# Gate and up of the feed-forward network in two blocks of 512 token pairs instead of three of 346 or 348, with the 32 sample tokens as separate fp32 products

## The chip, the cores and the metric

One core of one Trainium2 chip runs the whole program in a single launch. The metric is the device time of that launch in microseconds (us). Five engines work side by side, each with its own queue of instructions in a fixed order: PE (TensorE, the matrix multiplier; its weight loads are listed apart as PEld), ACT (ScalarE), DVE (VectorE), POOL (GpSimd), and SP, which here issues the DMA transfers. SBUF is the on-chip memory that all of them read, with 128 partitions; PSUM holds what PE writes; DRAM is the large memory outside, reached by DMA alone.

## The reference

One layer of an encoder is applied to 2048 prompt tokens and, with the same weights, to 32 sample tokens. All data are fp32, the model width is 1024, the hidden width of the feed-forward network 2816.

```
xp = xp + rmsnorm(mix_output(band_attention, gated_linear_attention))      # stage 1
xp = xp + rmsnorm(mem_attention(rmsnorm(xp)))                              # stage 2, 256 memory tokens
xp = xp + rmsnorm(swiglu(rmsnorm(xp, g_pre_ffn), w_gate, w_up, w_down))    # stage 3
swiglu(h) = (silu(h @ w_gate) * (h @ w_up)) @ w_down
```

The sample tokens go through the same three lines with cached keys, values and state. The change is in stage 3 and in the part of stage 2 that hands its result over.

## The kernel before

[...]

**Seven products.** The large products are made by a scheme with seven half-size products in place of eight: tokens are paired (a column of the operand is one token of the first half and one of the second), the width of 1024 is cut into two halves of 512, and seven sums of quarters (`seven_mov` for the tokens, `seven_sta` for the weights) are multiplied and added up. One unit is 7 products x 4 blocks of 128 rows x 3 = 84 matmuls, with as many columns as the block has token pairs.

**The stages by PE.** From 0 to about 151 us the first weights and tokens, to 545 us the combined projection, to 1159 us attention, gated recurrence and output projection, to 1387 us the memory scores (`ms`), to 1574 us the memory output (`mem_out`, PSUM tiles `mops`, four blocks of 512 tokens, weights `vw0` to `vw3`), to 2474 us gate and up (`gate_up`, PSUM tiles `pg_X`, `pg_Y`, `pg_Z` and `pu_X`, `pu_Y`, `pu_Z`), and then the down projection (`pdn`).

**Gate and up.** There are 1024 prompt pairs and 16 sample pairs. They go in three blocks (`CF = (348, 346, 346)`), and in each block over 11 groups `g` of 256 hidden columns. `unit_w` loads 1 MB of raw weights, forms the seven sums and splits them into 7 tiles (`wg_s` or `wu_s`); `unit` multiplies them with the block's seven operands `mf` and adds up on ACT and DVE; then silu, the product of both halves, and seven sums `u` for the down projection, which go to DRAM (`ud`). The operands of a block come from four raw tiles in SBUF (`hr`, the pool `cg`), which `ffn_raw` fills from DRAM: block 0 from already normed tokens (`h2d`), blocks 1 and 2 from `x2d`, multiplied by the gain and the row scale `r2d` on DVE. `ffn_ops` then makes the seven sums on DVE and splits each (cast 128x1384 on ACT, subtraction on DVE). Each `mf` tile exists once, so the next block's operand is written when the last product with the old one is done.

**Down.** `pdn` multiplies the seven sums `u` (tiles `ur`, 1 MB each, read from `ud`, split in place by `split_own`) in two halves of 512 pairs. The sample tokens' down products are plain fp32 products: `tail_down` takes the 32 tokens as weights of 32 columns, and four such matmuls stand side by side in PE (PSUM tile `utp`, line 2551).

**mem_out.** It norms its result twice (`n3` after the product, `n4` ahead of the network). For blocks 0 to 2 the squares are added up on DVE and one fp32 matmul with a matrix of ones sums over the partitions (line 2140); for block 3 (`BYTOK = 3`) each of the eight squares goes through such a matmul itself (line 2151).

**Order.** `Order` records all instructions, gives each a cost, and makes a plan by list scheduling in 60 passes; the plan sets the order on every engine, SP included, for the whole program. `shifted` moves a group's urgency, `whole` keeps PE instructions together.

**Addresses.** In the built program all weight tiles of gate and up and of down start 128 bytes past a multiple of 256 in their partition, the `ur` tiles on a multiple of 256, the rows of the `mf` tiles (348 x 4 bytes) at varying offsets. In `mem_out` the tiles `vw1` to `vw3` and all operands lie on multiples of 256; `vw0` lies 64 bytes past one.

Of the kernel before, what the change touches and what calls it, by code (L numbers as in the profile page):

```python
# [19 lines left out]
P = 128  # L20
# [28 lines left out]
class Order:  # L49
# [56 lines left out]
    def _cost(self, ins, kind, eng, outs, inps):  # L106

        n = self._free(outs[0])
        if eng == "PE":
# [10 lines left out]
            t = n * 0.4385 + 6.5  # L120
# [370 lines left out]
def encoder_step(ctx, tc, ins, outs):  # L491
# [16 lines left out]
    EARLY = 20000.0  # L508
    ident = cpool.tile([P, P], F32, name="ident")
# [115 lines left out]
    FIRST = 696  # L625
    h2d = [dpool.tile([D, min(n, FIRST - c0)], F32, name=f"h2d{b}") for b, (c0, n) in enumerate(CB) if c0 < FIRST]
    r2d = dpool.tile([P, T - FIRST], F32, name="r2d")
# [1192 lines left out]
    with ExitStack() as ph:  # L1820
# [273 lines left out]
        BYTOK = 3  # L2094

        def mem_out(b):
# [29 lines left out]
            def norm(name):  # L2126

                r = rs[0][:, 512 * (name == "n4") :][:, :n]
                if b >= BYTOK:
                    return norm_rows(name, r)  # L2130
                acc = row(f"{name}_{b}_acc")
# [9 lines left out]
                ACT.activation(r, ps, AF.Ln, bias=eps_t, scale=1.0 / D)  # L2141
                ACT.activation(r, r, AF.Exp, scale=-0.5)
                return r

            def norm_rows(name, r):

                ps = pn.tile([P, 512], F32, tag="norm", name=f"{name}_{b}_ps")
                for k in range(KT):
                    sq = copied(f"{name}_{b}_sq{k}")
                    ACT.activation(sq, y[k], AF.Square)  # L2150
                    PE.matmul(ps, lhsT=ones, rhs=sq, start=k == 0, stop=k == KT - 1)
# [19 lines left out]
            def fin_sample():  # L2171
                r = sample_norm("n3")
                xr = sample_small("xr_s").rearrange("p (k t) -> p k t", k=KT)
                SP.dma_start(xr, x1d[b][:, 512:].rearrange("(k p) t -> p k t", p=P))
# [3 lines left out]
                SP.dma_start(x2d[b][:, 512:].rearrange("(k p) t -> p k t", p=P), ys)  # L2178
                SP.dma_start(r2d[:, TP - FIRST :], sample_norm("n4"))

            def fin():
# [10 lines left out]
                hn = max(0, min(n, FIRST - s))  # L2192
                if hn < n:
                    SP.dma_start(r2d[:, s + hn - FIRST : s + n - FIRST], r[:, hn:])
                for k in range(KT):
                    if hn:
                        DVE.scalar_tensor_tensor(out=y[k][:, :hn], in0=y[k][:, :hn], scalar=gains["g_pre_ffn"][:, k : k + 1], in1=r[:, :hn], op0=ALU.mult, op1=ALU.mult)
                        SP.dma_start(h2d[b][k * P : (k + 1) * P, :], y[k][:, :hn])

            return [first] + ([fin_sample] if b == NB - 1 else []) + [partial(tile_m, m) for m in range(KT)] + [fin]  # L2200

        for b in range(NB):
            for it in mem_out(b):
                it()


    CF = (348, 346, 346)
    UN = 512
    TAIL = 330
    CTOK = [[[(0, 348)], [(348, 696)]], [[(696, 1042)], [(1042, 1388)]],  # L2210
            [[(1388, 1718), (TP, TP + 16)], [(1718, TP), (TP + 16, T)]]]
    CPUT = [[(0, 0, 348, 0)], [(0, 0, 164, 348), (1, 164, 346, 0)], [(1, 0, TAIL, 182)]]
# [6 lines left out]
    WRB, SGB = 4, 4  # L2219
    fps = ctx.enter_context(ExitStack())  # L2220
    pd, pt, pn = (fps.enter_context(tc.tile_pool(name=name, bufs=bufs, space=PSUM, **RW)) for name, bufs in (("cpd", 6), ("cpt", 1), ("cpn", 1)))
    with ExitStack() as ph:
# [3 lines left out]
        mps = {i: pool(f"cm{i}", 1) for i in (1, 2, 3, 4)}  # L2226
        sp = pool("cs", 4)
        mps[0] = pool("cm0", 1)
        gp = pool("cg", 4)
        wr = pool("cwr", WRB)  # L2230
        wsa = pool("cwa", 6)
        mps.update({i: pool(f"cm{i}", 1) for i in (5, 6)})
        wsb = pool("cwb", 6)

        def stage(name):
            return gp.tile([P, HK, 348], F32, tag="stage", name=name)

        scales = []

        def ffn_raw(b):  # L2240

            n = CF[b]
            raw, rows_ = {}, {}
            for kh, c in ((0, 0), (0, 1), (1, 1), (1, 0)):
                r = stage(f"hr{b}_{kh}{c}")
                at = 0
                for t0, t1 in CTOK[b][c]:
                    for bb, lo, hi, off in pieces(CB, t0, t1):
                        SP.dma_start(r[:, :, at + off : at + off + hi - lo], (x2d if b else h2d)[bb][kh * 512 : kh * 512 + 512, lo:hi].rearrange("(k p) n -> p k n", p=P))
                    at += t1 - t0  # L2250
                raw[kh, c] = r[:, :, :n]
                if b:
                    if c not in rows_:
                        rows_[c] = scales[0].tile([P, 348], F32, tag="rrow", name=f"rr{b}_{c}", bufs=2)[:, :n]
                        at = 0
                        for t0, t1 in CTOK[b][c]:
                            SP.dma_start(rows_[c][:, at : at + t1 - t0], r2d[:, t0 - FIRST : t1 - FIRST])
                            at += t1 - t0
# [469 lines left out]
```

## Time and profile before

| | |
|---|---|
| median of 3 runs | 2939.53 us (2936.64 to 2943.05) |
| the profiled execution | 2934.58 us, 4.95 us under the median |
| its span, first to last instruction | 2932.8 us, so 1.8 us lie outside it |
| gate and up, 1574.2 to 2474.0 us | 899.8 us, PE busy 896.51 us |
| matmuls of gate and up | 5544 in fp32r (3 blocks x 11 x 2 x 84) |
| matmuls of down | 1716 with 512 columns, 264 with 256 |
| granted PE clock, mean | 0.996 |

In the profile's rows, a group of instructions has its line, engine, operation, tiles (out<-in), shapes and count, then the busy time and the mean duration of one in ns, then the engine's idle time ahead of them and what ended it. Matmuls overlap each other, so their mean duration (381 ns) is longer than their distance from start to start. The distance, called pitch here, is read from stretches that hold nothing else: stretch by number of matmuls.

### The profile page before, as it was taken

What the parts mean: (1) busy time and instruction counts of PE and PEld (TensorE: products, weight loads), DVE (VectorE), ACT (ScalarE), POOL (GpSimd) and SP (SyncE); (2) the same over time, 40 slices, a digit from 0 to 9 for tenths busy, and PEclk for the clock granted to TensorE, in tenths of its full rate; (3) what the DMA queues carried; (4) which work ended last, traced back from release to release, by engine and by line L of the source; (5) the groups of instructions that cost most, each with busy time, mean ns of one, the idle gap of its engine ahead of it and who ended that gap; (6) DMA issues with size and microseconds to landing.
All of it is one profiled execution on the core that took longest, in us unless ns stands there. A gap on an engine that the chain in (4) does not pass through costs nothing.

```text
span 2932.8 us, 53153 instructions
## 1 busy us (share of the span) xinstructions
PE 2886.2 (98%) x19680; PEld 2623.7 (89%) x19680; DVE 2081.6 (71%) x3695; ACT 1572.5 (54%) x3205; POOL 671.4 (23%) x1002
## 2 busy tenths in 40 slices
PE   8999999999999999999999999999999999999999
PEld 8999999888888787887788999999999999778888
DVE  5677976576775757875558977888788876445565
ACT  5556555576785767676435544544455444333333
POOL 0202000377674746000001121121112211000013
PEclk9999999999999999999999999999999999999999
DMA  7556373885785857448446443454435444996566
GB/s 211 189 177 206 114 232 126 252 263 176 215 265 153 256 162 235 153 145 296 153 135 218 148 140 114 126 160 136 119 101 153 135 124 149 289 302 205 196 225 209
DMA packets 506982, 539.96 MB, mean 184 GB/s; under 512 B 63425, under 2 KB 399498, under 8 KB 506690
## 3 DMA queue, kind: packets, MB, share of 16 engines
q1 hardware_dynamic: 506722, 536.57, 58.1%
q8 instruction: 154, 2.52, 0.4%
q14 instruction: 106, 0.87, 0.1%
HBM read 387.36 MB, written 152.24 MB: 184 GB/s over the span
## 4 chain that ended last, share of the span: by engine, by line
PE 92%; DMA 2%; POOL 2%; DVE 1%; ACT 1%; issue 1%; SPq 0%; DVEq 0%; POOLq 0%; ACTq 0%
PE pdn L595 15%; PE pg_X L595 9%; PE pu_X L595 9%; PE mops L595 6%; PE wops L1556 4%; PE pg_Y L595 4%; PE pu_Y L595 4%; PE ms_X L595 3%; PE pu_Z L595 2%; PE pg_Z L595 2%; PE s L1235 2%; PE wva_X L595 2%; PE wops L595 2%; PE wr_X L595 2%; PE wka_X L595 2%; PE wvb_X L595 2%
## 5 line engine op out<-in xcount | busy, mean ns | idle before, releaser
L595 PE MATMUL pdn<-ur,wd_s 128*128 128x512 f32 (+1 forms) x1980 | 436.4, 381 | 0.0
L595 PEld LDWEIGHTS pdn<-ur,wd_s 128*128 128x128 f32 x1980 | 354.9, 188 | 78.5 <-issue 3.9
L595 PE MATMUL pg_X<-mf,wg_s 128*128 128x346 f32 (+1 forms) x1584 | 286.2, 322 | 1.5 <-ACT mf L527 1.2
L595 PE MATMUL pu_X<-mf,wu_s 128*128 128x346 f32 (+1 forms) x1584 | 284.9, 322 | 1.7 <-DVE up L647 1.7
L595 PEld LDWEIGHTS pg_X<-mf,wg_s 128*128 128x128 f32 x1584 | 258.1, 188 | 3.5 <-ACT mf L527 1.4
L595 PEld LDWEIGHTS pu_X<-mf,wu_s 128*128 128x128 f32 x1584 | 257.9, 188 | 3.2 <-DVE up L647 2.0
L527 ACT CAST wu_s<-wu_r 128x512 fp32r<-128x512 f32 x231 | 139.9, 622 | 158.5 <-DVE wu_r L644 85.0
L528 DVE TENSOR_TENSOR wg_s<-wg_r,wg_s 128x512 fp32r<-128x512 f32 x231 | 166.1, 735 | 33.4 <-ACT wg_s L527 33.1
L528 DVE TENSOR_TENSOR wu_s<-wu_r,wu_s 128x512 fp32r<-128x512 f32 x231 | 169.8, 744 | 20.9 <-ACT wu_s L527 19.7
L595 PE MATMUL mops<-mo,vw 128*128 128x512 f32 x768 | 183.1, 396 | 0.8 <-ACT y L2121 0.7
L647 POOL TENSOR_TENSOR wg_r<-wg_r,wg_r 128x512 f32<-128x512 f32 x33 | 46.7, 1415 | 570.1 <-PE n_s_ps L2163 395.3
L595 PEld LDWEIGHTS mops<-mo,vw 128*128 128x128 f32 x768 | 143.2, 188 | 35.4 <-issue 3.9
L527 ACT CAST wg_s<-wg_r 128x512 fp32r<-128x512 f32 x231 | 139.3, 620 | 53.0 <-DVE wg_r L644 37.7
L1556 PE MATMUL wops<-om,wo_s 128*128 128x512 f32 x576 | 152.4, 404 | 0.8 <-POOL om L533 0.6
L595 PE MATMUL pg_Y<-mf,wg_s 128*128 128x346 f32 (+1 forms) x792 | 142.3, 323 | 0.0
L595 PE MATMUL pu_Y<-mf,wu_s 128*128 128x346 f32 (+1 forms) x792 | 142.3, 322 | 0.0
L533 DVE TENSOR_TENSOR ur<-ur 128x2048 fp32r<-128x2048 f32 (+1 forms) x42 | 90.5, 2155 | 60.5 <-ACT ur L532 60.5
L532 ACT CAST ur<-ur 128x2048 fp32r<-128x2048 f32 (+1 forms) x42 | 74.1, 1764 | 107.3 <-DMA ur<-ud 107.3
L595 PEld LDWEIGHTS pg_Y<-mf,wg_s 128*128 128x128 f32 x792 | 128.8, 189 | 1.7 <-issue 1.4
L595 PEld LDWEIGHTS pu_Y<-mf,wu_s 128*128 128x128 f32 x792 | 129.0, 189 | 0.0
L647 POOL TENSOR_TENSOR wu_r<-wu_r,wu_r 128x512 f32<-128x512 f32 x33 | 46.2, 1401 | 359.6 <-DMA wu_r<-in_w_ffn_up_dram 216.3
L1556 PEld LDWEIGHTS wops<-om,wo_s 128*128 128x128 f32 x576 | 104.6, 188 | 24.0 <-POOL om L533 1.5
(598 smaller groups left out, 6749.1 us busy)
## 6 DMA issues: line engine op xcount, KB each, us to landing
wg_r<-in_w_ffn_gate_dram SPq DMA_DIRECT2D x66, 512.0 KB, 4.6
wu_r<-in_w_ffn_up_dram SPq DMA_DIRECT2D x66, 512.0 KB, 4.1
ur<-ud SPq DMA_DIRECT2D x28, 1024.0 KB, 6.7
wd<-in_w_dn_dram SPq DMA_DIRECT2D x72, 256.0 KB, 5.5
wo_r<-in_w_o_dram SPq DMA_DIRECT2D x64, 256.0 KB, 3.8
ud<-u SPq DMA_DIRECT2D x77, 174.0 KB, 2.2
ud<-u SPq DMA_DIRECT2D x77, 165.0 KB, 2.6
wdr<-in_w_dn_dram SPq DMA_DIRECT2D x22, 512.0 KB, 7.3
```

The costliest lines, as they stand in the source:

```text
L527: ACT.copy(hi, src)
L528: (lo_eng or DVE).tensor_tensor(out=lo, in0=src, in1=hi.bitcast(F32), op=ALU.subtract)
L532: ACT.copy(m[:, 0], m[:, 1].bitcast(F32))
L533: (POOL if on_pool else DVE).tensor_tensor(out=m[:, 1], in0=m[:, 1].bitcast(F32), in1=m[:, 0].bitcast(F32), op=ALU.subtract)
L595: PE.matmul(ps, lhsT=a, rhs=b, start=first and i == 0, stop=last and i == len(seq) - 1, skip_group_check=skip)
L647: eng.tensor_tensor(out=out, in0=a, in1=b, op=ALU.add)
L1235: PE.matmul(ps_out, lhsT=q[:, 2 * i + e, q0 : q0 + nq], rhs=ks[:, e, k0 : k0 + ncol], start=i == 0, stop=i == 1)
L1556: PE.matmul(ps, lhsT=a, rhs=b, start=i == 0, stop=i == len(seq) - 1)
```

## The change

Gate and up go in two blocks of 512 prompt pairs. The 32 sample tokens leave the blocks: `sample_rows` multiplies them as in `tail_down`, 176 fp32 matmuls of 256 columns in 12 groups, with the gate and up weights read once more as raw rows (`wt` tiles from the same ring as the raw weights). The seven operand sums of a block are kept in DRAM (`hop`): for block 0 `mem_out` makes them (`pair_operands`, in blocks 0 and 1), for block 1 `late_rows` makes them during the groups 2, 4, 6 and 8 of block 0. `ffn_ops` reads each sum straight into the low half of its `mf` tile (1 MB by one DMA) and splits it in place, by quarters; for the odd operands the subtraction is on POOL. The `hr` pool is gone. `norm_rows` is gone too: block 3 of `mem_out` adds its squares on DVE as the others do, and its last step is made more urgent. All copies of `mops` are on ACT. The plan's cost of a fp32r matmul is another straight line (231.0 to 227.1 ns at 512 columns, 118.7 at 256 as before), so the order changes in every stage.

The pools of stage 3 are laid out anew. In the built program every weight tile of gate and up and of down then starts on a multiple of 256 bytes; of the seven `mf` tiles six do (rows of 2048 bytes keep that), and `mf3` lies 64 bytes past one; so does the one ring of `ur` in its place (456 of the 1716 down matmuls with 512 columns).

```diff
-            t = n * 0.4385 + 6.5
+            t = n * 0.4235 + 10.3
...
+    def pair_operands(c, k, a11, a12, a22, a21):
+        r = slice(k * P, k * P + P)
+        sub(DVE, a11, a12, a11)
+        SP.dma_start(hop[c][1][r], a11)
+        sub(DVE, a12, a22, a12)
+        SP.dma_start(hop[c][4][r], a12)
+        SP.dma_start(hop[c][3][r], a22)
+        sub(DVE, a11, a22, a11)
+        SP.dma_start(hop[c][2][r], a11)
+        sub(DVE, a21, a21, a11)
+        SP.dma_start(hop[c][6][r], a21)
...
-                    (ACT.copy if m % 2 else DVE.tensor_copy)(y[m], ps)
+                    ACT.copy(y[m], ps)
...
-                if b >= BYTOK:
-                    return norm_rows(name, r)
...
-                        SP.dma_start(h2d[b][k * P : (k + 1) * P, :], y[k][:, :hn])
+                    if b == 0:
+                        SP.dma_start(hop[0][5 * (k // HK)][k % HK * P : k % HK * P + P], y[k])
+                if b == 1:
+                    for k in range(HK):
+                        t = quad(rp, "rows", f"hp{k}").rearrange("p (k n) -> p k n", k=2)
+                        for h in range(2):
+                            SP.dma_start(t[:, h], hop[0][5 * h][k * P : k * P + P])
+                        pair_operands(0, k, t[:, 0], y[k], y[HK + k], t[:, 1])
...
-    CF = (348, 346, 346)
...
-            seven_mov(raw, put)
+            for i in range(7):
+                m_ = mps[i].tile([P, 2, HK, UN], F32R, tag="mov", name=f"mf{b}_{i}")
+                SP.dma_start(m_[:, 1].bitcast(F32), hop[b][i].rearrange("(k p) n -> p k n", p=P))
+                for k in range(HK):
+                    split_own(m_[:, :, k], i % 2 == 1)
+                ops.append((m_[:, 0], m_[:, 1]))
...
+        def sample_rows():
...
+                            with issue_order.whole():
+                                for k, t in rows:
+                                    for j in range(nj):
+                                        PE.matmul(ps[j * TS : (j + 1) * TS, i * 256 : i * 256 + 256], lhsT=hs[:, k], rhs=t[:, j * 256 : j * 256 + 256], start=k == 0, stop=k == KT - 1, skip_group_check=True)
...
+        def late_rows():
...
+                for i, (c, kh) in enumerate(((0, 0), (1, 0), (1, 1), (0, 1))):
+                    kk = k + kh * HK
+                    SP.dma_start(v[i], x2d[2 + c][kk * P : kk * P + P, :512])
+                    DVE.scalar_tensor_tensor(out=v[i], in0=v[i], scalar=gains["g_pre_ffn"][:, kk : kk + 1], in1=r[c], op0=ALU.mult, op1=ALU.mult)
+                for i, o in ((0, 0), (3, 5)):
+                    SP.dma_start(hop[1][o][k * P : k * P + P], v[i])
+                pair_operands(1, k, *v)
...
+        for b in range(2):
+            for g in range(NG):
+                gate_up(b, g, side)
+                if b == 0 and g in (2, 4, 6, 8):
+                    next(rows_)
+                if b + g and g < NG - 1 and (b or g % 2 == 0):
+                    next(side, None)
+            if b == 0:
+                ops = ffn_ops(1)
```

How the plan moves instructions is seen at three places. In the rows the shape behind a matmul is that of its output, a number behind a tile's name tells its instance, and `x12` is the number of equal instructions in a row.

The first place is PE at the end of `mem_out` and the start of gate and up. Before:

```order
L595 MATMUL mops_7_19678<-mo_1_19449,vw_18408 128x512 x12
L2151 MATMUL n_3_ps<-n_3_sq_19705,ones 128x512
L2151 MATMUL n_3_ps<-n_3_sq_19708,ones 128x512
L595 MATMUL pg_0_X<-mf_0_19939,wg_0_s_19984 128x348 x12
L2151 MATMUL n_3_ps<-n_3_sq_19711,ones 128x512
L595 MATMUL pg_0_Y<-mf_1_19943,wg_0_s_19989 128x348 x12
L595 MATMUL pg_0_X<-mf_2_19948,wg_0_s_19993 128x348 x11
L2151 MATMUL n_3_ps<-n_3_sq_19714,ones 128x512
L2151 MATMUL n_3_ps<-n_3_sq_19717,ones 128x512
```

The same place in the change:

```order
L596 MATMUL mops_7_19740<-mo_1_19540,vw_18422 128x512 x12
L2150 MATMUL n_2_ps<-n_2_acc,ones 128x512
L596 MATMUL pg_0_X<-mf_0_20023,wg_0_s_20104 128x512 x9
L2150 MATMUL n_3_ps<-n_3_acc,ones 128x512
L596 MATMUL pg_0_X<-mf_0_20023,wg_0_s_20104 128x512 x3
L596 MATMUL pg_0_Y<-mf_1_20033,wg_0_s_20109 128x512 x12
L596 MATMUL pg_0_Z<-mf_5_20073,wg_0_s_20123 128x512 x11
```

Of the sixteen matmuls `n_3_ps` that stood between the first products of gate and up, two are left, and the second matmul of block 2 (`n_2_ps`) has moved here.

The second place is PE where one block of gate and up ends and the next begins (group 10 of the old block, then group 0 of the new one). Before, with `mf_0_23116` the new block's first operand:

```order
L595 MATMUL pu_10_Z<-mf_5_19957,wu_10_s_22992 128x348 x11
L595 MATMUL pg_0_X<-mf_0_23116,wg_0_s_23152 128x346
L595 MATMUL pu_10_Z<-mf_5_19957,wu_10_s_22992 128x348
L595 MATMUL pg_0_X<-mf_0_23116,wg_0_s_23152 128x346 x3
L595 MATMUL pu_10_X<-mf_6_19961,wu_10_s_22995 128x348 x12
L595 MATMUL pg_0_X<-mf_0_23116,wg_0_s_23152 128x346 x8
L595 MATMUL pg_0_Y<-mf_1_23120,wg_0_s_23157 128x346
```

In the change, with `mf_0_23401` the new block's first operand:

```order
L596 MATMUL pu_10_Z<-mf_5_20073,wu_10_s_23277 128x512 x12
L596 MATMUL pu_10_X<-mf_6_20083,wu_10_s_23280 128x512 x12
L596 MATMUL pg_0_X<-mf_0_23401,wg_0_s_23482 128x512
L596 MATMUL pg_0_Y<-mf_1_23411,wg_0_s_23487 128x512 x12
L596 MATMUL pg_0_X<-mf_0_23401,wg_0_s_23482 128x512 x5
L596 MATMUL pu_0_X<-mf_0_23401,wu_0_s_23611 128x512
L596 MATMUL pg_0_X<-mf_0_23401,wg_0_s_23482 128x512
L596 MATMUL pu_0_X<-mf_0_23401,wu_0_s_23611 128x512
L596 MATMUL pg_0_X<-mf_0_23401,wg_0_s_23482 128x512 x5
L596 MATMUL pu_0_X<-mf_0_23401,wu_0_s_23611 128x512 x5
L596 MATMUL pg_0_Z<-mf_5_23451,wg_0_s_23501 128x512
```

There is one such passage instead of two, and the new block's products no longer begin before the old block's last one.

The third place is where the new block's operands come from at that passage. Before, DVE makes their sums out of the raw tiles `hr` in SBUF (line 644) and their low parts (line 528):

```order
L528 TENSOR_TENSOR mf_3_23128<-hr_11_22537,mf_3_23128 128x4x346
L528 TENSOR_TENSOR mf_1_23120<-hr_00_22520,mf_1_23120 128x4x346
L644 TENSOR_TENSOR hr_00_22520<-hr_11_22537,hr_00_22520 128x4x346
L644 TENSOR_TENSOR hr_01_22529<-hr_11_22537,hr_01_22529 128x4x346
L528 TENSOR_TENSOR mf_2_23125<-hr_00_22520,mf_2_23125 128x4x346
```

In the change the queue of SP holds in their place the seven transfers out of DRAM, with those of the sample tokens' raw weights (`wtup`) in between:

```order
L2378 DMA wtup_0_23755<-in_w_ffn_up_dram 128x1024
L2267 DMA mf_0_23401<-hop_0_133 128x4x512
L2378 DMA wtup_1_23757<-in_w_ffn_up_dram 128x1024
L2267 DMA mf_1_23411<-hop_1_134 128x4x512
L2267 DMA mf_2_23421<-hop_2_135 128x4x512
L2267 DMA mf_3_23431<-hop_3_136 128x4x512
L2267 DMA mf_4_23441<-hop_4_137 128x4x512
L2267 DMA mf_5_23451<-hop_5_138 128x4x512
L2378 DMA wtup_2_23759<-in_w_ffn_up_dram 128x1024
L2267 DMA mf_6_23461<-hop_6_139 128x4x512
L2378 DMA wtup_3_23761<-in_w_ffn_up_dram 128x1024
```

Each of the seven waits on SP until PE has done the last product with the old operand in its tile, and what stands behind it in SP's queue waits with it.

More of the change, by code (lines that the diff above doesn't have):

```diff
@@ L2233, in encoder_step @@
[L2233 to L2258, printed above, removed]
-                    for kk in range(HK):
-                        v = raw[kh, c][:, kk]
-                        DVE.scalar_tensor_tensor(out=v, in0=v, scalar=gains["g_pre_ffn"][:, kh * HK + kk : kh * HK + kk + 1], in1=rows_[c], op0=ALU.mult, op1=ALU.mult)
-            return raw
@@ L2479, in residual @@
             if halves:
-                xr = [xa.tile([P, HK, UN], F32, tag="A", name=f"{name}_{kh}") for kh in range(2)]
+                xr = [xa["A"].tile([P, HK, UN], F32, tag="A", name=f"{name}_{kh}") for kh in range(2)]
             else:
@@ L2633, in encoder_step @@
                     continue
-                ps = [pd.tile([P, 512], F32, tag="dense", name=f"pdn{i}_{c}_{m}") for m in range(HK)]
+                ps = [bank(f"pdn{i}_{c}_{m}") for m in range(HK)]
                 for q in range(len(GC)):
```

321 lines of the change are left out of this document (175 added, 146 removed).

## The prediction

> **What bounds the kernel now.** I read the busy shares first, then the chain of waits, then the windows by stage, and last the timeline of PE at the places that the change touches. From the page:
>
> ```profile
> span 2932.8 us, 53153 instructions
> PE 2886.2 (98%) x19680; PEld 2623.7 (89%) x19680; DVE 2081.6 (71%) x3695; ACT 1572.5 (54%) x3205; POOL 671.4 (23%) x1002
> PE 92%; DMA 2%; POOL 2%; DVE 1%; ACT 1%; issue 1%; SPq 0%; DVEq 0%; POOLq 0%; ACTq 0%
> ```
>
> PE is busy for 98% of the span and makes up 92% of the chain. The windows say where: each row has a stretch, its length, the busy time of the engines with their instructions, the granted clock, the DMA share and GB/s.
>
> ```profile
> core 0: us, PE busy (x) PEld busy (x) DVE busy (x) ACT busy (x) POOL busy (x), PEclk, DMA share, GB/s
> 545.00:1159.00 614.00, 588.58 (x5970) 499.89 (x5969) 420.47 (x1105) 439.73 (x1134) 412.83 (x799) 0.99 0.71 217
> 1381.00:1574.20 193.20, 192.45 (x886) 152.44 (x885) 122.72 (x199) 86.07 (x151) 1.29 (x1) 1.00 0.51 174
> 1574.20:2474.00 899.80, 896.51 (x5576) 888.07 (x5575) 739.51 (x1121) 439.10 (x833) 174.97 (x129) 1.00 0.45 136
> 1630.00:1890.00 260.00, 260.00 (x1633) 260.00 (x1633) 211.50 (x326) 121.33 (x233) 49.39 (x38) 1.00 0.40 125
> 1900.00:2185.00 285.00, 285.00 (x1794) 284.96 (x1793) 237.65 (x369) 135.93 (x262) 58.71 (x44) 1.00 0.46 133
> 2200.00:2473.50 273.50, 273.50 (x1722) 273.50 (x1721) 215.17 (x329) 129.15 (x248) 54.92 (x40) 1.00 0.45 138
> 2640.00:2826.00 186.00, 186.00 (x802) 150.78 (x801) 103.69 (x129) 58.53 (x68) 0.00 (x0) 1.00 0.59 195
> ```
>
> In gate and up PE is idle for 3.3 of 899.8 us, and not at all inside the three blocks (the fourth to sixth row): 818.5 us for 5149 matmuls, a pitch of 159.0 ns at 346 or 348 columns. The clock is full. So time there can only go by fewer or cheaper matmuls, and a pause of PE is paid in full. Down (the last row) has 231.9 ns at 512 columns.
>
> Whether 512 columns cost that much in gate and up is the main unknown. `mem_out` has the same shape:
>
> ```profile
> 1442.10:1447.69 5.59, 5.59 (x25) 4.51 (x24) 5.33 (x9) 3.63 (x7) 0.00 (x0) 1.00 0.44 125
> 1447.70:1453.14 5.44, 5.44 (x25) 4.50 (x24) 4.98 (x9) 1.69 (x4) 0.00 (x0) 1.00 0.96 355
> 1493.30:1525.95 32.65, 32.65 (x145) 27.03 (x144) 17.72 (x28) 8.21 (x14) 0.00 (x0) 1.00 0.34 107
> ```
>
> The first is 24 matmuls with the weight tile `vw0`, the second 24 with `vw1` on the same operand, the third 144 with `vw1` to `vw3`; each count holds one matmul that only reaches in. The pitches are 233, 226.7 and 226.7 ns. DMA traffic doesn't explain the first: its DMA share is 0.44, the faster second one's 0.96. What differs is that `vw0` starts 64 bytes past a multiple of 256. Down's weights start 128 past, and its pitch is near that of `vw0`. I take it that a weight tile off 256 costs 5 to 7 ns per matmul. That is an inference from two stages, not a shown cause.
>
> **The change, part by part.**
>
> *Fewer, longer matmuls.* Gate and up lose 5544 x 159.0 = 881.5 us and get 2 x 11 x 2 x 84 = 3696 matmuls of 512 columns. Every weight tile is now on 256, as `vw1` is; six operands in seven are too, and `mf3` is not. I take 227.5 ns for six sevenths and 233.3 for the seventh: 228.3 on average, 843.9 us. That is **-37.6 us**. Ends: 226.7 everywhere gives -43.6, 233.3 everywhere -19.2.
>
> *Sample tokens.* 176 fp32 matmuls in 12 groups of 16 or 12, four side by side. Down has such a group:
>
> ```profile
> 2534.16 1.09 PE L595 MATMUL pdn<-ur,wd_s 128*128 128x512 f32 x4
> 2535.18 1.93 PE L2551 MATMUL utp<-wdr,ut 128*32 128x256 f32 x32
> 2537.05 1.20 PE L595 MATMUL pdn<-ur,wd_s 128*128 128x512 f32 x4
> ```
>
> From its start to the next `pdn` are 1.87 us for 16 matmuls (two records each); the four `pdn` ahead take 1.02 us rather than 4 x 0.232 = 0.93, and I add as much behind: 2.07 us. Twelve are 24.8, and a few transposes 0.7: **+25.5 us** (24 to 28), all on PE's path. The weights are read once more as raw rows, but two blocks read them twice instead of three times, so the traffic is as before.
>
> *The norm of block 3.* Its fp32 matmuls with ones stand among the first products of gate and up:
>
> ```profile
> 1601.72 0.48 PE L595 MATMUL pu_X<-mf,wu_s 128*128 128x348 f32 x2
> 1602.03 1.02 PE L2151 MATMUL n_ps<-n_sq,ones 128*128 128x512 f32 x2
> 1602.49 2.00 PE L595 MATMUL pu_X<-mf,wu_s 128*128 128x348 f32 x9
> 1604.32 0.32 PE L595 MATMUL pu_Z<-mf,wu_s 128*128 128x348 f32 x1
> L2151 PE MATMUL n_ps<-n_sq,ones 128*128 128x512 f32 x32 | 15.2, 591 | 0.0
> L647 DVE TENSOR_TENSOR n_acc<-n_acc,n_sq 128x512 f32<-128x512 f32 x42 | 28.8, 690 | 29.0 <-ACT n_sq L2137 25.0 <-ACT n_acc L2134 1.7 <-DVE n_acc L647 0.5
> ```
>
> 1601.72 to 1604.32 are 2.60 us for 11 products (11 x 0.159 = 1.75) and one fp32 matmul, which so takes 0.85. Sixteen such (32 records) become two: 14 x 0.85 = **-11.9 us**. In their place come 14 additions of 690 ns on DVE, which has 70 us free in `mem_out` (the 193.2 us row). If they were late, the first product of gate and up would wait; that is in the passage's term.
>
> *Down.* 1260 of the 1716 matmuls with 512 columns have both operands on 256 afterwards: 1260 x (231.9 - 227.5) = **-5.5 us** (0 to -6.6).
>
> *Passages and covers.* PE's pauses in gate and up, from the timeline (in brackets the idle time and what ended it):
>
> ```profile
> 1621.11 2.81 PE L595 MATMUL pu_X<-mf,wu_s 128*128 128x348 f32 x16 [1.75 <-DVE up L647]
> 1895.59 0.42 PE L595 MATMUL pg_X<-mf,wg_s 128*128 128x346 f32 x1 [0.38 <-ACT pg_c L686]
> 2191.21 0.43 PE L595 MATMUL pg_X<-mf,wg_s 128*128 128x346 f32 x1 [1.15 <-ACT mf L527]
> ur<-ud SPq DMA_DIRECT2D x28, 1024.0 KB, 6.7
> L532 ACT CAST mo<-mo 128x512 fp32r<-128x512 f32 x32 | 18.5, 617 | 0.1
> L533 DVE TENSOR_TENSOR mo<-mo 128x512 fp32r<-128x512 f32 x32 | 20.6, 686 | 5.6 <-ACT mo L532 4.3 <-DMA wor<-in_w_mo_dram 1.3
> L533 POOL TENSOR_TENSOR om<-om 128x512 fp32r<-128x512 f32 x24 | 32.8, 1387 | 4.8 <-ACT om L532 4.3
> ```
>
> Both block passages together cost 1.5 us. The new one is another thing: `mf_0` must be freed by the old block's last product with it, 1 MB must come from DRAM (6.7 us, as `ur` does), and a quarter must be split (0.6 + 0.7 us). By PE's new order at least 72 matmuls of old products (16.4 us) stand behind that release, so `mf_0` fits. The last two operands have 25 and 39 us after it, and an odd one is split on POOL in 4 x 1.39 = 5.5 us. At the start of gate and up the operands take the same way, block 0's behind its pair sums. For both I take **+3 us** net; ends -3 (all hidden) and +12 (two loads with their first split, 8 us each, seen three quarters). Behind the waiting loads in SP's queue stand raw weights; these are fetched some groups ahead.
>
> Inside a block DVE is the nearest cover. It is busy 664.3 of 818.5 us, 21.7 us in the 26.7 that a group of 168 matmuls takes; if all of it grew with the columns it would be 32.0 us, in a group of 168 x 0.2283 = 38.4. The weights' splits don't grow, so it has more room than before, and ACT (47%) too. Moving all `mops` copies to ACT falls in a stage where ACT is busy 86 of 193 us: 0.
>
> *Order elsewhere.* The plan is made anew. PE's largest pauses are in the stretch 545 to 1159 us, 25.4 us; a new order may win or lose some of it: 0 (-5 to +5).
>
> **Sum:** -37.6 + 25.5 - 11.9 - 5.5 + 3 = **-26.5 us**. The profiled execution (2934.58) comes to 2908.1; it lies 4.95 under the median, which comes to **2913.0**.
>
> **The rivals.**
>
> 1. *Addresses don't matter*, and gate and up go at down's 231.9 ns: 857.1 us, -24.4; down 0. Sum -24.4 + 25.5 - 11.9 + 3 = -7.8: 2931.7. For it: down is the long stage of 512 columns and is steady. Against it: 5.59 and 5.44 us above, for the same operand and count. [...] Chance 0.13.
>
> 2. *The cost goes with the columns*, so that fewer matmuls save nothing: 159.0 / 346.7 = 0.459 ns a column, 234.8 ns at 512, 867.9 us, -13.6. Sum -2.5: 2937.0, no change. Against it: no 512-column row is that slow. [...] Chance 0.06, with that case in it.
>
> 3. *Slower: the passage starves.* The seven operands (7.3 MB) and, by the new order of SP, 3.8 MB of weights must come in the 39 us until the last operand is needed. At the 355 GB/s of the `vw1` row that is 31 us and fits. At the stage's own 138 it would be 80, so PE waits 41 us, and the sum is +14.5: 2954. It is slower than before by over 5.9 us when the wait exceeds 32.4 us, which is a rate under 155 GB/s. For it: one queue of SP issues everything, and a 1 MB load by itself lands at 157 GB/s. Against it: in the stage's rows 136 GB/s come at a DMA share of 0.45, so the stage asks for no more; the loads can run side by side. Chance 0.08.
>
> **How the numbers follow.** About 0.2% (5.9 us) can be told from no change. The main case has 0.70, with its own range 2900 to 2922: the pitch between 226.7 and 230 ns, the passage -3 to +12, the order 5 either way. Rival 1 counts two thirds as faster, rival 2 as no change, rival 3 as slower; 0.03 is left for an order of the other stages that is worse by more than 20 us. Faster 0.78, same 0.12, slower 0.10. The range goes to rival 1 and stops short of rivals 2 and 3: 2898 to 2934.
>
> **What would show it.** In the changed profile gate and up should take some 870 us, with a pitch of 226.7 to 230 ns in stretches without fp32; at 232, rival 1; at 235, rival 2. Twelve fp32 groups of some 2.07 us should stand there; above 2.5 that term is wrong. The group `n_ps` at the start of gate and up should have four records instead of 32. The pitch of `pdn` should fall towards 228 where `ur` is on 256. The one passage and the start should cost under 12 us of idle PE; a wait of 20 us or more ended by a DMA to `mf` is rival 3. If 0 to 1159 us moves by more than 5 us, the new order did it, which I cannot foresee.

## The result, and the profile after

The change runs in 2900.25 us (median of 4, 2899.23 to 2903.03) against 2941.24 us before (median of 4): a ratio of 0.9864, 95% interval 0.9847 to 0.9882, so 41 us faster where 26.5 were forecast, and inside the range of 2898 to 2934, near its lower end. Run again beside three variants it gave 2900.14 us (0.9862, 0.9844 to 0.9879).

The two profiled executions lie closer to each other than the medians: 2934.58 us before, 6.7 under that median, and 2903.03 after, 2.8 above it. They differ by 31.5 us, and only these can be placed in the trace. The rest is the scatter of executions, which goes with the granted clock: of 17 executions of the kernel before that stand beside rows384 below, the two with a mean clock of 0.997 took 2934.39 and 2936.20 us, the one with 0.993 took 2945.44. The two profiled ones had 0.996 and 0.994; 0.002 of 2900 us is 5.8 us, an estimate of what the change's trace lost by it.

From the page of the change:

```profile
span 2901.2 us, 49346 instructions
PE 2856.5 (98%) x18162; PEld 2442.1 (84%) x18162; DVE 1888.6 (65%) x3366; ACT 1497.7 (52%) x2996; POOL 649.6 (22%) x982
```

PE still bounds the kernel, with 29.7 us less to do. The windows, with the same columns as in the prediction: the first stretch before gate and up; gate and up; a part of it without fp32 groups; down; a part of it.

```profile
545.00:1159.00 614.00, 591.55 (x5966) 500.06 (x5966) 417.88 (x1106) 438.87 (x1130) 412.60 (x799) 0.98 0.71 218
1572.16:2442.71 870.55, 870.27 (x4061) 705.26 (x4059) 541.44 (x785) 354.62 (x592) 136.81 (x97) 1.00 0.49 159
1700.00:1760.00 60.00, 60.00 (x265) 49.45 (x264) 37.06 (x56) 23.52 (x40) 6.77 (x5) 1.00 0.44 145
2442.71:2901.24 458.53, 447.73 (x2239) 368.75 (x2237) 247.96 (x309) 151.71 (x197) 41.94 (x26) 0.99 0.70 234
2640.00:2790.00 150.00, 150.00 (x661) 123.68 (x660) 86.72 (x108) 47.78 (x55) 0.00 (x0) 1.00 0.57 192
```

Gate and up begin at 1572.2 us (1574.2 before) and take 870.6 instead of 899.8, with 0.3 us of idle PE instead of 3.3. The pitch is 227.3 ns there (60 us for 264 matmuls) and the same in down (150 us for 660), which had 231.9. Down as a whole, cut at its first matmul, hardly gained. This is the same stretch in the kernel before:

```profile
2473.59:2932.81 459.22, 452.98 (x2240) 368.58 (x2239) 250.67 (x312) 155.21 (x199) 43.57 (x26) 1.00 0.72 235
```

459.2 to 458.5 us: PE is busy for 5.3 us less and idle for 4.6 us more (10.8 instead of 6.2). The timeline of PE in down shows the new pauses, in brackets; below them are ACT's cast and DVE's subtraction of a `ur` tile, ahead of the second pause:

```profile
2635.89 1.19 PE L596 MATMUL pdn<-ur,wd_s 128*128 128x512 f32 x4 [0.50 <-ACT ur L533]
2638.22 155.08 PE L596 MATMUL pdn<-ur,wd_s 128*128 128x512 f32 x680 [1.13 <-DVE ur L534]
2852.93 1.22 PE L596 MATMUL pdn<-ur,wd_s 128*128 128x256 f32 x4 [2.88 <-ACT ur L533]
...
2633.93 1.91 ACT L533 CAST ur<-ur 128x2048 fp32r<-128x2048 f32 x1 [3.41 <-DMA ur<-ud]
2635.87 2.29 DVE L534 TENSOR_TENSOR ur<-ur 128x2048 fp32r<-128x2048 f32 x1 [1.79 <-ACT ur L533]
```

PE stands ready and waits for the split of the next operand: 4.5 us in three places. The kernel before had no such pause in `pdn`. At the longest of them the clock falls too:

```profile
2852.60:2856.00 3.40, 3.07 (x14) 3.07 (x15) 3.09 (x3) 2.29 (x3) 0.00 (x0) 0.50 0.92 272
```

For 3.4 us the granted clock is 0.50: the four products of 256 columns take 1.02 us there, to the next matmul at 2853.95, where at a full clock 121 of them take 14.51 (2877.94 to 2892.45). So by an estimate half of PE's 3.07 us there, 1.5, are lost beyond the pause itself. The experiments have more of this.

In gate and up, the timeline shows the fp32 group of the sample tokens, the matmuls `n_ps` at the start (the first is the one of block 2 that has moved here, the other two are those that remain of block 3's sixteen), and four products of one unit (x12 is four blocks of 128 rows by the three matmuls in fp32r that make one fp32 product: high part by high, high by low and low by high):

```profile
1571.70 1.02 PE L2150 MATMUL n_ps<-n_acc,ones 128*128 128x512 f32 x2
1574.64 1.02 PE L2150 MATMUL n_ps<-n_acc,ones 128*128 128x512 f32 x2
1615.38 1.02 PE L2150 MATMUL n_ps<-n_acc,ones 128*128 128x512 f32 x2
...
1689.27 1.93 PE L2383 MATMUL tsgate<-wtgate,hs 128*32 128x256 f32 x32
1691.14 3.01 PE L596 MATMUL pg_X<-mf,wg_s 128*128 128x512 f32 x12
...
2133.74 2.93 PE L596 MATMUL pg_Y<-mf,wg_s 128*128 128x512 f32 x12
2136.50 2.93 PE L596 MATMUL pg_X<-mf,wg_s 128*128 128x512 f32 x12
2139.27 2.88 PE L596 MATMUL pg_Z<-mf,wg_s 128*128 128x512 f32 x12
2141.99 2.88 PE L596 MATMUL pg_X<-mf,wg_s 128*128 128x512 f32 x12
```

The group takes 1.87 us from start to start, as in down. From one start to the next, the last four rows show 2.76 us for `mf3` (230 ns per matmul), 2.77 for `mf4` (231) and 2.72 for `mf5` (226.7).

At the passage the queue of SP shows the seven transfers, and the window how fast data came:

```profile
1986.46 0.37 SPq L2267 DMA_DIRECT2D mf<-hop  x1
1990.09 11.33 SPq L2267 DMA_DIRECT2D mf<-hop  x5
2003.78 0.36 SPq L2267 DMA_DIRECT2D mf<-hop  x1
1990.00:2010.00 20.00, 20.00 (x90) 16.44 (x89) 16.69 (x19) 16.02 (x30) 11.79 (x9) 1.00 1.02 373
mf<-hop SPq DMA_DIRECT2D x14, 1024.0 KB, 7.4
```

For 20 us the DMA share is 1.02, at 373 GB/s, and PE is busy for all 20.00 us. Rival 3 named the right place, but the rate rose to 373 GB/s there, where it took the stage's 138.

### The profile page after: what moved, and what is told of

It is laid out like the page before. It is cut to its first block, busy times and chain, and to the rows that moved or that the text cites. A ratio compares the mean times of both kernels' runs of the same rounds, so it can differ in the third digit from the quotient of the medians.

```text
span 2901.2 us, 49346 instructions
## 1 busy us (share of the span) xinstructions
PE 2856.5 (98%) x18162; PEld 2442.1 (84%) x18162; DVE 1888.6 (65%) x3366; ACT 1497.7 (52%) x2996; POOL 649.6 (22%) x982
## 4 chain that ended last, share of the span: by engine, by line
PE 58%; DMA 1%; POOL 0%; ACT 0%; DVE 0%; issue 0%; DVEq 0%; ACTq 0%; POOLq 0%
PE pdn L596 13%; PE pg_X L596 8%; PE pu_X L596 8%; PE mops L596 6%; PE pg_Y L596 4%; PE pu_Y L596 4%; PE ms_X L596 3%; PE pg_Z L596 2%; PE pu_Z L596 2%; PE wops L596 2%; PE ms_Y L596 2%; PE ms_Z L596 1%; PE mpt L2007 0%; PE tsgate L2383 0%; PE tsup L2383 0%; PE utp L2592 0%
## 5 line engine op out<-in xcount | busy, mean ns | idle before, releaser
L596 PE MATMUL pg_X<-mf,wg_s 128*128 128x512 f32 x1056 | 262.2, 393 | 0.0
L596 PE MATMUL pu_X<-mf,wu_s 128*128 128x512 f32 x1056 | 258.8, 390 | 0.0
L596 PEld LDWEIGHTS pg_X<-mf,wg_s 128*128 128x128 f32 x1056 | 197.4, 188 | 47.4 <-issue 6.0
L596 PEld LDWEIGHTS pu_X<-mf,wu_s 128*128 128x128 f32 x1056 | 198.3, 188 | 42.1
L529 DVE TENSOR_TENSOR wu_s<-wu_r,wu_s 128x512 fp32r<-128x512 f32 x154 | 107.7, 702 | 145.8 <-ACT wu_s L528 141.9
L529 DVE TENSOR_TENSOR wg_s<-wg_r,wg_s 128x512 fp32r<-128x512 f32 x154 | 111.7, 727 | 99.3 <-ACT wg_s L528 98.1
L528 ACT CAST wu_s<-wu_r 128x512 fp32r<-128x512 f32 x154 | 95.2, 621 | 142.9 <-PE pg_X L596 51.4
L596 PE MATMUL pg_Y<-mf,wg_s 128*128 128x512 f32 x528 | 130.0, 391 | 0.0
L596 PE MATMUL pu_Y<-mf,wu_s 128*128 128x512 f32 x528 | 129.9, 391 | 0.0
L1249 PE MATMUL s<-ks,qbuf 128*128 128x256 f32 (+2 forms) x448 | 112.7, 342 | 4.3 <-DVE u_mn L1224 3.9
```

The costliest lines, as they stand in the source:

```text
L528: ACT.copy(hi, src)
L529: (lo_eng or DVE).tensor_tensor(out=lo, in0=src, in1=hi.bitcast(F32), op=ALU.subtract)
L596: PE.matmul(ps, lhsT=a, rhs=b, start=first and i == 0, stop=last and i == len(seq) - 1, skip_group_check=skip)
L1249: PE.matmul(ps_out, lhsT=q[:, 2 * i + e, q0 : q0 + nq], rhs=ks[:, e, k0 : k0 + ncol], start=i == 0, stop=i == 1)
```

## The experiments

The theory after the result: the pitch of 227 ns comes from the addresses, the fewer matmuls make the rest, and the other terms of the sum hold as worked out. The rivals: the address is not the cause; the layout alone would have done it; the small terms are not what was put down. The kernel before had medians of 2941.24 us beside w128, all256, oldcost and the repeated change (2900.14), 2938.43 beside before256, before_acc, no_sample and quarters, and 2939.96 beside the other four; the ratios are to these, and a distance from the change's 2900.14 that crosses the groups is uncertain by some 3 us.

**w128: the weights' address undone.** In the pools of gate and up:

```diff
+        pad("cpad2", 128)
         wsc = pool("cwc", 2)
+        pad("cpad3", 128)
         mps[2] = pool("cm2", 1)
+        pad("cpad4", 128)
         wsa = pool("cwa", 3)
...
-        pad("cpad0", 2624)
+        pad("cpad0", 2240)
```

> The change with five of the seven weight tiles of gate and up moved 128 bytes off a multiple of 256 (two stay on it, as a control inside the run); nothing else is meant to differ, though the plan makes a somewhat different order. Theory (the address of the weight tile sets the pitch): the 2640 matmuls with a moved tile take 231 to 233 ns in quiet stretches, the 1056 others stay at 227 to 230, gate and up grow from 870.5 by 2640 x 4.5 = 12 us, the whole to some 2912. Rival (the faster pitch comes from the stage, the order or the banks): all stay at 227 to 230 and the whole stays within 4 us of the change's 2900.

2912.72 us (0.9905, 0.9891 to 0.992), 12.6 above the change beside it. Gate and up, and four products in the order `mf2`, `mf3`, `mf4`, `mf5`:

```profile
1570.39:2455.26 884.87, 884.87 (x4061) 707.17 (x4059) 541.34 (x785) 353.90 (x592) 135.78 (x97) 1.00 0.47 156
...
2138.21 2.96 PE L596 MATMUL pg_X<-mf,wg_s 128*128 128x512 f32 x12
2141.00 2.92 PE L596 MATMUL pg_Y<-mf,wg_s 128*128 128x512 f32 x12
2143.76 2.94 PE L596 MATMUL pg_X<-mf,wg_s 128*128 128x512 f32 x12
2146.54 2.95 PE L596 MATMUL pg_Z<-mf,wg_s 128*128 128x512 f32 x12
```

From start to start, `mf2` with a moved weight tile takes 2.79 us (232.5 ns; 226.7 is what aligned products have in the change), `mf3` with its tile left alone 2.76 as in the change, and `mf4`, also left alone, 2.78 (231.7 ns; 2.77 in the change). So the products with a moved tile rose by 5 to 6 ns from the change to this run and the two others stayed within 1, all at a full clock; inside the run alone the two kinds differ less, since `mf3` and `mf4` are slow for another reason (all256 below). That the weights' address sets 5 to 6 ns of the pitch at 512 columns is shown. Down is a control too: its weights stayed on 256, and 680 of its products take 155.04 us, as in the change (155.08).

**all256: the last tiles on 256.**

```diff
-        pad("cpad0", 2624)
+        pad("cpad0", 2560)
-        pad("cpad1", 704)
+        pad("cpad1", 768)
...
-        pad("dpad0", 3648)
+        pad("dpad0", 3584)
-        pad("dpad1", 704)
+        pad("dpad1", 768)
```

> The change with four pads altered by 64 bytes, so that mf3 and the fourth ur ring also start on a multiple of 256; every engine has the same instructions in the same order. Theory (the address of the moving operand counts too, about half as much as that of the weights): mf3 falls from 230.2 to 227.5 ns (528 matmuls, -1.4 us), down's 456 from 229.8 to 227.4 (-1.1 us): 2.5 us less in all. Rival (only the weights' address counts): no change.

2895.44 us (0.9847, 0.9832 to 0.9862), 4.7 below the change. `mf3`, `mf4`, `mf5` and `mf6`, then the long row of down:

```profile
2126.11 2.88 PE L596 MATMUL pg_Y<-mf,wg_s 128*128 128x512 f32 x12
2128.83 2.88 PE L596 MATMUL pg_X<-mf,wg_s 128*128 128x512 f32 x12
2131.55 2.88 PE L596 MATMUL pg_Z<-mf,wg_s 128*128 128x512 f32 x12
2134.27 2.88 PE L596 MATMUL pg_X<-mf,wg_s 128*128 128x512 f32 x12
...
2627.41 154.44 PE L596 MATMUL pdn<-ur,wd_s 128*128 128x512 f32 x680 [0.81 <-DVE ur L534]
```

All products take 2.72 us. The moving operand's address counts too, and `mf4` gained with `mf3` although only `mf3` was moved. Over 1056 matmuls (both operands, 88 products of 12 each) that is 1056 x 3.8 ns = 4.0 us; PE's busy time in gate and up fell by 4.2 us (870.3 to 866.1), and with 0.7 us more of idle time the stage from 870.6 to 867.1. The 680 matmuls of down fell from 155.08 to 154.44. The intervals of the two ratios overlap, so the whole's gain rests on these rows.

**oldcost: the plan's cost line put back.**

```diff
-            t = n * 0.4235 + 10.3
+            t = n * 0.4385 + 6.5
```

> The change with the plan's old cost line for a fp32r matmul; same instructions and addresses, another order. Theory (what the stages before gate and up and down gained or lost is the order's chance): gate and up stay within 2 us of 870.5, the whole moves by up to 5 us either way. Rival (the new line is worth something by itself): the whole is over 6 us slower than the change.

2902.12 us (0.9869, 0.9852 to 0.9885), 2 above the change, within its scatter; gate and up 872.1 us by PE's first matmuls, 1.5 more. The new line is not shown to be worth anything.

**before256 and rows384: the layout without the new blocks.** Both start from the kernel before; one moves its weight tiles, the other pads its operand rows, which puts the weights on 256 too:

```diff
+        pool("cpadw", 1).tile([P, 32], F32, name="cpadw")
         wsa = pool("cwa", 6)
```

```diff
-                m_ = mps[len(ops)].tile([P, 2, HK, 348], F32R, tag="mov", ...)
+                m_ = mps[len(ops)].tile([P, 2, HK, 384], F32R, tag="mov", ...)
```

> The kernel before with one pad of 128 bytes, so that all weight tiles of gate and up start on a multiple of 256 (its operands keep their rows of 1392 bytes at changing offsets; the plan makes another order). This asks how much of the gain the layout would have given without new blocks. Theory A (a moved weight tile costs some 5 ns per matmul at any number of columns): the pitch falls from 159.0 to 154, gate and up by 28 us, the whole to 2913. [...] Theory C (the operands' odd rows set the pitch): nothing. Down, whose weights stay 128 off, keeps 232 ns.

> The kernel before, its blocks of 348 and 346 pairs as they are, but the mf tiles with rows of 1536 bytes instead of 1392, so that every operand row and every weight tile of gate and up starts on a multiple of 256 (the plan makes another order). before256 left the pitch at 159, so the weights' address alone is worth nothing with rows at odd offsets. Theory A (either operand off 256 costs some 5 ns per matmul, once): pitch 153 to 154, gate and up 28 to 32 us shorter, the whole near 2908, so most of the gain was the layout's. [...]

before256: 2936.02 us (0.9993, 0.998 to 1.0005). rows384: 2961.73 us (1.0077, 1.006 to 1.0093). One quiet stretch of each, before256 first:

```profile
1920.00:2180.00 260.00, 260.00 (x1637) 260.00 (x1637) 215.32 (x338) 124.55 (x242) 53.49 (x41) 1.00 0.44 131
1920.00:2180.00 260.00, 260.00 (x1632) 260.00 (x1631) 218.75 (x344) 119.97 (x238) 52.17 (x41) 1.00 0.47 139
```

260 us for 1636 and 1631 matmuls: 158.9 and 159.4 ns, where the kernel before has 159.0. At 346 columns the address is worth nothing, neither of the weights nor of the operands. At 256 columns it isn't either: down's products take 119.4 ns before (107 from 2911.29 to 2924.07 us), with their weights 128 past, and 119.9 in the change (121 from 2877.94 to 2892.45). A missed in both; C was right on before256, but its cause, the odd rows, falls with rows384. So the layout pays only at 512 columns, of the three lengths seen here. That the weight loads set the pitch at 346 columns, where PEld is busy for the whole 260 us, is ruled out by the same 256-column products: they load as many weights each and start 119 to 120 ns apart. A line through 159.0 ns at 346.7 columns (the mean of the three blocks) and 226.7 at 512 has 0.41 ns a column and 17 ns a matmul, an estimate of what each matmul that falls away is worth; through 119.9 at 256 columns and 226.7 it is 0.42 and 13, so the estimate holds to some 4 ns. rows384 lost 22 us in another way: its PE idles for 14.0 us in gate and up and 12.0 in down, where the kernel before has 3.3 and 6.2, at a clock of 0.99. Its longest pauses are 5.85 and 3.67 us, and the clock is 0.50 for 3.4, 6.8 and 6.8 us at 1595.2, 1615.7 and 2516.8 us, with PE busy for 13.2 us of that. The 16.5 us more of idle time and half of these 13.2 make some 23 of the 27 us that the two stages lost, an estimate. Why its order has these pauses was not settled.

**before_acc, acc_urgent and no_urgency: the norm of block 3.** The first is the kernel before with its sixteen matmuls replaced:

```diff
-        BYTOK = 3
+        BYTOK = 4
...
-                acc = row(f"{name}_{b}_acc")
+                acc = (copied if b == NB - 1 else row)(f"{name}_{b}_acc")
```

> The kernel before with the norm of block 3 done as for the other blocks: its squares are added up on DVE, two matmuls with ones instead of sixteen. Theory (the 14 matmuls stand on PE's path at 0.85 us each): 11.9 us less, all of it in the first 50 us of gate and up. Rival (PE would have waited there anyway, for operands or weights): pauses take their place and the whole moves by less than 4 us.

2942.59 us (1.0014, 1.0005 to 1.0023): not 12 us faster but slightly slower (by 4, at the rival's edge). Its gate and up, the pause that did it, and the clock at that pause:

```profile
1575.85:2481.16 905.31, 890.13 (x5548) 885.86 (x5549) 739.70 (x1130) 438.86 (x830) 170.84 (x129) 0.99 0.44 135
1623.26 2.08 PE L2140 MATMUL n_ps<-n_acc,ones 128*128 128x512 f32 x2 [11.38 <-DVE n_acc L647]
1615.10:1632.20 17.10, 8.18 (x23) 6.61 (x24) 14.58 (x25) 10.97 (x17) 1.86 (x3) 0.50 0.56 188
```

PE is busy for 6.4 us less than before (890.1 against 896.5) and idle for 15 instead of 3. The one matmul behind seven additions stands in PE's fixed order, and all products behind it wait 11.4 us for DVE. Around the pause the clock is one half for 17.1 us, in which PE is busy for 8.2: some 4 us lost, an estimate, and most of why PE's busy time fell by 6.4 and not by 11.9. The second adds the change's urgency:

```diff
-            for it in mem_out(b):
+            items = mem_out(b)
+            for it in items[:-1]:
                 it()
+            with issue_order.shifted(-40000.0 * (b == NB - 1)):
+                items[-1]()
```

> before_acc (two matmuls with ones for block 3 instead of sixteen) with the last step of mem_out made more urgent, as the change has it. In before_acc PE waited 11.4 us in front of such a matmul for DVE's additions, which the plan had put late. Theory (the wait comes from the place of the additions in DVE's order, not from a lack of DVE): the wait falls under 3 us and the whole comes to 8 to 10 us under the kernel before, some 2930. Rival (DVE has no room there in the kernel before): a wait of 5 us or more remains, here or at the first products, and the whole stays within 4 us of the kernel before.

2942.78 us (1.0012, 1.0002 to 1.0021). The 11.4 us are gone, and others are there (the clock is 0.50 for 6.8 us at 1589.2 and again at 1602.9 us):

```profile
1592.12 3.27 PE L595 MATMUL pg_Y<-mf,wg_s 128*128 128x348 f32 x10 [4.08 <-DVE mf L528]
1601.45 0.58 PE L595 MATMUL pu_Y<-mf,wu_s 128*128 128x348 f32 x2 [2.16 <-ACT wu_s L527]
1604.21 3.27 PE L595 MATMUL pg_X<-mf,wg_s 128*128 128x348 f32 x10 [2.17 <-DVE sg L647]
```

The rival holds: in the kernel before, DVE and ACT bound the first 50 us of gate and up, and the sixteen matmuls stood largely in time that PE would have idled anyway. Gate and up idles for 10.8 us of 901.5 here, 7.5 more than before, and half of the 9.4 us that PE is busy at the halved clock are, by an estimate, most of the rest. The third takes the urgency out of the change:

```diff
-    LAST_FIN = 40000.0
+    LAST_FIN = 0.0
```

> The change without the added urgency of the last step of mem_out (LAST_FIN = 0). Theory: the wait that before_acc showed comes up here too, 5 to 12 us of idle PE in the first 60 us of gate and up, the whole 2905 to 2912. Rival (the longer products of 512 columns cover it): gate and up as in the change, 2900.

2907.08 us (0.9891, 0.9876 to 0.9906), 7 above the change: the whole that the theory gave, with a shorter wait than it gave:

```profile
1620.90 2.08 PE L2150 MATMUL n_ps<-n_acc,ones 128*128 128x512 f32 x2 [3.28 <-DVE n_acc L661]
```

Gate and up take 877.2 us, 6.6 more than in the first trace of the change. Of these 3.5 are idle time, and the clock is 0.50 for 6.8 us from 1620.3, with PE busy for 6.2, so that some 3.1 (an estimate) are the clock's; in the trace the whole is no longer than the change's, because earlier stages came out shorter in that execution. The urgency is worth some 6 us in gate and up; what it is worth in the whole was not settled.

**no_sample: the fp32 groups taken out.**

```diff
+            for f in range(NF):
+                SP.dma_start(utd[f], hs[:, f % KT])
+            yield
-            for cbs in ((0, 1), (2,)):
+            for cbs in ():
```

> The change without the gate and up products of the 32 sample tokens (their hidden values are filled from the normed tokens by 22 small transfers instead, so this computes less): prices the 12 fp32 groups. Theory (each group costs 2.07 us on PE's path, and the transposes 0.7): 25.5 us less than the change, 2874.5, gate and up 845. Rival (the groups also disturb their neighbours and the weights' transfers): 30 us less or more. Other rival (part of it lay in pauses): less than 20.

2881.53 us (0.9807, 0.979 to 0.9824), 18.6 below the change. Gate and up, and the longest pause in it:

```profile
1568.16:2419.51 851.35, 845.82 (x3701) 693.85 (x3700) 541.78 (x782) 353.71 (x589) 139.81 (x97) 1.00 0.41 135
1593.08 0.73 PE L596 MATMUL pu_Y<-mf,wu_s 128*128 128x512 f32 x2 [2.37 <-ACT wu_s L528]
```

PE is busy for 24.5 us less (870.3 to 845.8), as priced, but 5.5 us of pauses come in, most of them at the start, for splits on ACT and DVE. With another order, 19 us were on the path: the second rival, at its edge.

**double_load: the passage under twice the load.**

```diff
-                SP.dma_start(m_[:, 1].bitcast(F32), hop[b][i]...)
+                for _ in range(2 if b else 1):
+                    SP.dma_start(m_[:, 1].bitcast(F32), hop[b][i]...)
```

> The change with each of the seven operand transfers at the one passage issued twice, 14.7 MB instead of 7.3 (the computation is the same). It asks how near the passage is to starving PE. In the change the transfers ran at 373 GB/s and took 20 us of the 39 there are, with no idle PE. Theory (the margin is 15 to 20 us, and the second load of 1 MB at 373 GB/s takes 2.8 us for each operand): 20 us more of transfers, PE idle for at most 5 us, the whole within 5 us of the change. Rival (each operand's own path of release, transfer and split has no such margin, since the transfers stand in one queue): 10 to 20 us of idle PE at the passage, the whole 2910 to 2920.

2907.54 us (0.989, 0.9875 to 0.9905), 7 above the change, between the theory's 5 and the rival's 10. 1980 to 2020 us and the longest pause:

```profile
1980.00:2020.00 40.00, 35.80 (x149) 27.16 (x148) 26.52 (x34) 17.28 (x31) 11.84 (x8) 1.00 0.94 348
2001.17 0.51 PE L596 MATMUL pg_X<-mf,wg_s 128*128 128x512 f32 x1 [1.18 <-ACT mf L533]
```

PE idles for 4.2 of these 40 us, in many short pauses. Twice the bytes cost 4 to 7 us: the passage has room, though not twice its need. The theory's bound on the idle time held.

**quarters: the new wait in down.** all256, and:

```diff
-                    split_own(m_, False)
+                    for k in range(g1 - g0):
+                        split_own(m_[:, :, k], False)
```

> The change with mf3 and the fourth ur ring on 256 as in all256, and down's operands split by quarters of 512 columns instead of in one piece of 2048 (ACT 1.9 us and DVE 2.3 us in a row). Theory (the new pauses of some 4 us in down stand before the first matmul on a ur tile that is split too late): the first quarter is ready after 1.3 instead of 4.2 us, PE's idle time in down falls from 10 to 6 or 7 us, the whole by 3 to 4 us below all256's 2895. Rival (the transfer itself is late): no change; or the longer sum of the four splits makes it slower.

2889.53 us (0.9833, 0.9816 to 0.985), the fastest here, 10.6 below the change and 5.9 below all256. Down (its order, too, came out somewhat different):

```profile
2437.80:2888.59 450.79, 444.25 (x2239) 367.67 (x2237) 257.76 (x415) 161.04 (x300) 37.79 (x26) 0.99 0.71 238
```

6.6 us less than all256's 457.4, with 6.5 us of idle PE instead of 10.1, and no pause for a `ur` tile left in the timeline. The other 3.1 us are mostly the clock's: all256 pauses for 2.40 us ahead of 2840.45 and then has a clock of 0.50 for 6.8 us, with PE busy for 6.2 (half of it is an estimate of the loss); here the clock stays full until the kernel's last 5 us. The result fits the theory but doesn't show it alone, since the order differs. In oldcost, with the split in one piece, another order is enough: down takes 454.1 us there with 8.2 us of idle PE, and 864 products follow each other where the change has its first two pauses.

## Why the prediction was right, and where not

The direction, the main term and the mechanism held; the sum came out 5 us short in the trace (31.5 against 26.5) and 14.5 short in the medians. That the sum lies so close in the trace is in part luck: up to down's first product gate and up fell by 28.8 us where its terms give 21.0, down by 0.7 where 5.5 was forecast, and the stages ahead by 2.0 where nothing was. "A pause of PE is paid in full" was also short of what the runs show: at a long one the clock was halved on top (0.50 for 3.4 us at the 2.88 us pause of the change, for 17.1 us at the 11.38 us one of before_acc).

- *Fewer, longer matmuls, -37.6.* Right. Leaving out those next to an fp32 group, the 3696 matmuls average 228.0 ns, 842.7 us or -38.8. The inference from `vw0` was confirmed by w128. At the 232.5 ns of a moved tile the term would be 881.5 - 859.3 = 22.2, so the layout gave 16.6 of it and the fewer matmuls 22.2. Some 12 of these 22.2 are the columns of the sample pairs, which left the blocks (29,568 columns at 0.41 ns, an estimate): that gain belongs beside the sample tokens' cost below. Only `mf3` was mis-sized (230 instead of 233.3), and `mf4` was not foreseen.
- *Sample tokens, +25.5.* PE's time was right (24.5), its share on the path less (19), since without them the start of gate and up waits for splits.
- *The norm, -11.9.* This step failed. "14 x 0.85" took PE's busy time for time on the path. The runs show that in the kernel before it was not: replacing the matmuls gained nothing, since pauses (15 us of idle PE in before_acc instead of 3) and the halved clock around them (0.50 for 17.1 us) took the time's place. In the change the time did go: PE is busy for all of the first 68 us of gate and up. That the urgency has a part in it is shown by no_urgency; that DVE has no operand sums to make there, and that the products are half as long again, are the likely other reasons, which no run tests. The term can't be added to the others.
- *Down, -5.5.* The pitch fell as forecast (231.9 to 227.3), but idle time grew by 4.6 us, nearly all of it waits for `ur` splits, and the halved clock took some 1.5 more. The step that was left out is whether the split of 4.2 us stays covered in the new order: in oldcost, at the same pitch, down takes 454.1 us, 5.1 less than before, close to the forecast gain. That PE's faster pace plays a part is likely, and not shown.
- *Passages, +3.* Mis-sized: idle time in gate and up fell by 3.0 us. The priced load and split were hidden, at both places.
- *Order elsewhere, 0.* Gate and up began 2.0 us earlier; with identical orders (the change twice, all256) that point lay at 1572.2, 1575.9 and 1566.6 us, so this is scatter.

Rival 1 is out by w128. Rival 2 is out, since the 512-column products of gate and up average 228.0 ns, not 234.8. What its chance of 0.06 holds besides is shown by no run: the best rows here, all on 256, stay at 226.7 ns. Rival 3 is out by the 373 GB/s row. The missing 10 us between trace and medians are the two executions' place in their scatter. Some 6 of them are the clock's, by the estimate above, and the rows show part of it: a clock of 0.98 against 0.99 between 545 and 1159 us, of 0.99 against 1.00 in down.

## What to carry to other kernels

Read the pitch of one shape in every stage that has it; where it differs at a full clock, compare the operands' addresses before costing a layout (232.5 against 226.7 ns at 512 columns here, and no difference at 346). A matmul's busy time is on the path only if PE would not wait there without it: look at what the next products need before counting it as a gain. A pause of the matrix engine can cost more than its length: read the granted clock in the microseconds around it (0.50 for 17.1 us at the 11.38 us pause of before_acc). After speeding up the bounding engine, look for the operand that now comes late; splitting its preparation into pieces, as in quarters, or another order, as in oldcost, may give the time back.

## What the runs showed of the hardware

- At 512 columns of fp32r, weights 128 bytes past a multiple of 256 cost 5.8 ns per matmul (232.5 against 226.7), a moving operand 64 past about 3 (230 against 226.7); at 346 columns neither shows (159.0 ns before, 158.9 in before256, 159.4 in rows384), and at 256 the weights' doesn't (119.4 and 119.9).
- The product after a shifted operand was slow as well (`mf4`, 231 ns) and recovered with it (226.7); the runs don't show why.
- At these pauses of PE in gate and up or down the granted clock was 0.50 for a while: 3.4 us at pauses of 2.53 (the repeated change) and 2.88 us (the change), 6.8 at 2.40 (all256), 3.28 (no_urgency), 4.08 (acc_urgent), 3.67 and 5.85 (rows384), 17.1 at 11.38 (before_acc). At a pause of 2.37 us (no_sample) it stayed full. At pauses of 2.16 and 2.17 us that stand close together it was 0.50 for 6.8 us (acc_urgent), at two of 1.07 and 1.53 us for 3.4 (rows384).
- While seven loads of 1 MB stood in SP's queue, all traffic together moved at 373 GB/s for 20 us; such a load landed after 7.4 us (median of 14).
